# A hybrid layer on one core: eleven matmuls on zeros ahead of the first product, GLU sums and head copies in another order, and an output projection in the order 3 to 7, 0, 1, 2 that keeps its last three tiles of x1 in SBUF

## The chip, the cores and the metric

The kernel runs on one core of a Trainium2 chip. A core has five engines with a queue each, in which instructions run in order: TensorE (PE), VectorE (DVE), ScalarE (ACT), GpSimd (POOL) and SyncE (SP). SP issues most DMA transfers here and POOL the rest; a transfer whose condition is not yet met holds up all that stand behind it in the queue that issues it. The metric is the device time of the whole program in microseconds (us), as the median of several executions.

## The reference

One layer with a residual stream x of 1024 tokens by 1024 channels, in three steps (float32 throughout):

```python
# 1. token mixing
h = rms_norm(x, mix_pre_g); proj = h @ w_in            # u (512), q, k, v (8 heads x 64), f_logit (8)
y_ssm = s5_mixer(u, ...)     # diagonal state space, y + d*u, g = gelu(y), g * sigmoid(g @ glu_w + glu_b)
y_fox = forgetting_attention(q, k, v, f_logit)         # causal, decay from cumsum(log_sigmoid(f))
y_mix = concat([rms_norm(y_ssm, ssm_out_g), rms_norm(y_fox, fox_out_g)])
x = x + rms_norm(y_mix @ w_out, mix_post_g)            # x1
# 2. cross-attention, 4 heads, into 256 memory tokens
x = x + rms_norm(memory_cross_attention(rms_norm(x, xa_pre_g), rms_norm(mem, mem_g), wq, wkv, wo), xa_post_g)
# 3. SwiGLU, 2816 hidden channels
h = rms_norm(x, ffn_pre_g)
x = x + rms_norm((silu(h @ w_gate) * (h @ w_up)) @ w_down, ffn_post_g)
```

## The kernel before

Tokens stand in eight tiles of 128. A float32 operand of a large product is split into a rounded part and a rest (`split`, L112: a copy on ACT, a subtraction on DVE, L113 and L115 or L117), and each product is three matmuls (`mm3`, L121: L122, L123, L124). The Python code traces instructions with priorities; a scheduler of the framework then sets the order on every engine with a timing model of its own, from the priorities, the data and the buffers that become free. So the order on an engine is not that of the code, an edit anywhere can move other instructions, and `tc.issue_after(i)` ties instructions of a block behind instruction `i` on the same engine. A tile pool hands out a fixed number of buffers for a tag (L193 for the front: `a` 2, `b` 2, `c` 3, `d` 1, `e` 1, `yt` 2); PSUM has four banks with the tag `g`, and two double banks `s` that become four banks `x` after the attention.

The stages in order of time:

- **Input projection, state-space part** (to about 60 us, L895 to L926). `x_fetch` loads the eight row tiles of the transposed x, `x_split` splits them, `u_load` loads and splits the weight of the same row, `u_part` adds 24 matmuls into eight banks. The first x tile is loaded in two halves, and the weight after them.
- **q, k, v and the state space** (to about 230 us): `in_proj` (L868), beside which `ssm` steps. `ssm_out` (L629) makes the output of the state space in two halves of four PSUM banks, each followed by a Gelu on ACT (L639), while tiles of the second half of v (`v_tiles`, L294, emptied by ACT L310) are interleaved.
- **Forgetting attention** (`fox`, L694, to about 498 us): for each head, `prepare` loads q, k and the decay and copies and splits them (L715, L716, L718); for each of eight query tiles, `scores` (L725; L733, L734, DVE L740, exponential ACT L742, scaling L747), `turn` (L750: transposes L764, copied to SBUF by DVE L767 or ACT L769 in turn), and for pairs of heads `values` (L771). `behind` (L722) ties a head's copies behind the last exponential so far; for the first head there is none. Between these steps the generator `fillers` (L962) is paced in: the rest of v, the GLU (`glu`, L653), the first part of the output projection (`out_ssm`, L826, whose rows L836 scales with the statistics r_s from `token_sums`, L233, and `rsqrt_mean`), the memory's keys and values, and half of a folded cross-attention weight (`build_a`). At the end of `glu`, `token_sums` adds up the squares with matmuls against a column of ones (L237); `glu_stats` (L688) turns the sums into r_s.
- **Output projection, attention part** (L1018 to L1040, about 498 to 566 us): for each token tile j, x and the first part of the sum (`t`, from t1_d, L1024) are loaded, eight `mm3` make the product, DVE L1031 scales and adds, ACT L1033 squares, POOL L1035 multiplies with the gain, and L1039 makes x1, which POOL's queue stores to x1_d (L1040). Beside it steps the second half of the folded weight.
- **Cross-attention** (to about 778 us): `xa_prep(j)` loads x1 of tile j (L1058) into a buffer with the tag `c`, squares it (L1061) and makes its statistics; scores, values and the feed-forward input follow. The loads are listed in `x1_read`, and `wd_sums` (L1324) ties copies of w_down in DRAM behind entries of that list.
- **Feed-forward** (to 1414 us): seven-product schemes for gate and up (`gate_up`) and for down (`DOWN`, L1505). `take`, `quarter` and `finish` empty the banks of the last products; the last one is tile (1, 3), whose lower half is squared on ACT (L1453) and multiplied with the gain on POOL (L1459), after which the statistics (L137 to L145) and the last addition (L1497) run.

The order of the output projection's buffers is set by these lines:

```python
xt = tt("c")
sp.dma_start(out=xt, in_=a["x"][ts, :])
t = tt("aab"[j % 3])
...
stC.dma_start(out=x1_d[j], in_=xt)
```

## Time and profile before

| | |
|---|---|
| time, median of 3 runs | 1423.64 us (1420.83 to 1426.41) |
| the profiled execution's own time | 1424.64 us |
| span of its profile, first to last instruction | 1422.9 us, mean granted TensorE clock 0.989 |
| busy in the span | PE 97%, weight loads 82%, DVE 67%, ACT 46%, POOL 29% |
| DMA | 234.22 MB moved, 165 GB/s on average |

The profile is of one execution. In a timeline row stand the start, the time, engine and line, operation, output and input tiles, and in brackets how long the engine had been idle before and what ended that. In a row of windows stand the stretch, then busy time and count of PE, PEld (weight loads), DVE, ACT and POOL, the granted clock, the busy share of DMA, and GB/s. SPq is SP issuing a transfer. Tiles bear the names of their buffers, so `a`, `b`, `c`, `g`, `x` are tags; a line such as L113 or L122 can be that of a helper with many callers.

### The profile page before, as it was taken

To read this page: it belongs to the slowest core of one execution; us is meant where nothing else is said; L and a number is where in the kernel's file an instruction comes from. 1 tells how busy PE (TensorE), PEld (TensorE's weight loads), DVE (VectorE), ACT (ScalarE), POOL (GpSimd) and SP (SyncE) were. 2 spreads that over 40 slices of the span, in tenths; PEclk is the share of its full clock that TensorE was granted. 3 is DMA by queue.
4 is the path that set the end of the run, shared out by engine and by line. 5 is a ranking of instruction groups with operands and counts; after the bars stand their busy time and mean duration, and the time that the engine had idled before them with its cause. 6 is when DMAs were issued, how large, how long until landed. Compare 5 with 4: busy or idle time off the path is not lost.

```text
span 1422.9 us, 20364 instructions
## 1 busy us (share of the span) xinstructions
PE 1380.0 (97%) x7342; PEld 1165.1 (82%) x7342; DVE 956.9 (67%) x1703; ACT 653.7 (46%) x1293; POOL 406.0 (29%) x428
## 2 busy tenths in 40 slices
PE   7999989899999898999999999999999999999997
PEld 6889889789888686788888788888888888888886
DVE  8839945956566676645457677787777676565565
ACT  6372336666676555533434533333333334544351
POOL 0001000013333134002021367687666661000021
PEclk9999999999999998999999999999999999999999
DMA  6324653155643758324537355554444446965544
GB/s 208 95 77 134 172 177 105 58 166 178 202 146 106 183 184 249 116 74 135 176 115 258 123 185 185 179 172 164 151 156 155 170 148 228 346 210 192 178 163 163
DMA packets 110230, 234.22 MB, mean 165 GB/s; under 512 B 11816, under 2 KB 46632, under 8 KB 110000
## 3 DMA queue, kind: packets, MB, share of 16 engines
q1 hardware_dynamic: 94496, 179.91, 39.8%
q0 software_dynamic: 15632, 53.00, 10.4%
q8 instruction: 58, 0.95, 0.3%
q14 instruction: 44, 0.36, 0.1%
HBM read 166.81 MB, written 74.71 MB: 170 GB/s over the span
## 4 chain that ended last, share of the span: by engine, by line
PE 59%; DVE 1%; ACT 0%; issue 0%; DVEq 0%; ACTq 0%
PE x L1260 17%; PE g L1260 13%; PE x L1518 7%; PE g L1518 7%; PE x L123 2%; PE x L124 2%; PE x L122 2%; PE g L122 2%; PE g L123 2%; PE g L124 2%; PE g L1048 1%; PE g L1156 1%; DVE slab L115 0%; DVE whl L115 0%; DVE c L1039 0%; DVE rst L141 0%
## 5 line engine op out<-in xcount | busy, mean ns | idle before, releaser
L1260 PE MATMUL x<-slab,op 128*128 128x512 f32 x984 | 233.2, 389 | 0.5 <-DVE op L115 0.5
L1260 PEld LDWEIGHTS x<-slab,op 128*128 128x128 f32 x984 | 184.7, 188 | 39.2 <-DVE op L115 1.0
L1260 PE MATMUL g<-slab,op 128*128 128x512 f32 x744 | 178.7, 389 | 0.0
L115 DVE TENSOR_TENSOR slab<-slab 128x1024 fp32r<-128x1024 f32 (+2 forms) x92 | 110.5, 1207 | 84.6 <-ACT slab L113 82.6
L1260 PEld LDWEIGHTS g<-slab,op 128*128 128x128 f32 x744 | 139.7, 188 | 28.9
L122 PE MATMUL g<-slab,whl 128*128 128x512 f32 (+1 forms) x416 | 151.5, 364 | 1.7 <-ACT t L958 1.3
L124 PE MATMUL g<-slab,whl 128*128 128x512 f32 (+1 forms) x416 | 148.6, 358 | 0.0
L123 PE MATMUL g<-slab,whl 128*128 128x512 f32 (+1 forms) x416 | 148.5, 357 | 0.0
L113 ACT ACTIVATE slab<-slab 128x1024 fp32r<-128x1024 f32 (+2 forms) x92 | 95.0, 1037 | 105.0 <-DMA slab<-hs_d 75.0
L1518 PE MATMUL g<-slab 128*128 128x512 f32 x462 | 126.7, 389 | 0.0
L1518 PE MATMUL x<-slab 128*128 128x512 f32 x462 | 126.7, 389 | 0.0
L1518 PEld LDWEIGHTS x<-slab 128*128 128x128 f32 x462 | 86.7, 188 | 18.0
L1518 PEld LDWEIGHTS g<-slab 128*128 128x128 f32 x462 | 86.7, 188 | 18.0
L122 PE MATMUL g<-whl,slab 128*128 128x256 f32 (+2 forms) x288 | 88.5, 313 | 8.3 <-ACT whl L113 7.3
L115 DVE TENSOR_TENSOR whl<-raw,whl 128x1024 fp32r<-128x1024 f32 (+2 forms) x61 | 71.5, 1175 | 30.9 <-ACT whl L113 30.6
L115 DVE TENSOR_TENSOR op<-slab,op 128x512 fp32r<-128x512 f32 x80 | 83.4, 1053 | 11.5 <-ACT op L113 11.3
L1336 POOL TENSOR_TENSOR wt<-wt 128x256 f32<-128x256 f32 x88 | 83.5, 949 | 21.3 <-DMA wt<-in_w_down 17.7
L122 PEld LDWEIGHTS g<-slab,whl 128*128 128x128 f32 x416 | 78.6, 189 | 12.9 <-ACT t L958 1.5
L124 PEld LDWEIGHTS g<-slab,whl 128*128 128x128 f32 x416 | 78.4, 189 | 11.6 <-DVE whl L115 0.2
L123 PEld LDWEIGHTS g<-slab,whl 128*128 128x128 f32 x416 | 78.6, 189 | 10.6
L124 PE MATMUL g<-whl,slab 128*128 128x256 f32 (+2 forms) x288 | 86.9, 302 | 0.0
L123 PE MATMUL g<-whl,slab 128*128 128x256 f32 (+2 forms) x288 | 86.8, 301 | 0.0
(384 smaller groups left out, 2903.2 us busy)
## 6 DMA issues: line engine op xcount, KB each, us to landing
hs_d<-ev POOLq DMA_DIRECT2D x77, 256.0 KB, 2.6
slab<-hs_d SPq DMA_DIRECT2D x35, 512.0 KB
wt<-in_w_down SPq DMA_DIRECT2D x44, 256.0 KB
wt_d<-wt POOLq DMA_DIRECT2D x22, 512.0 KB, 4.8
slab<-in_w_gate SPq DMA_DIRECT2D x20, 512.0 KB
slab<-in_w_up SPq DMA_DIRECT2D x20, 512.0 KB
slab<-wt_d SPq DMA_DIRECT2D x20, 512.0 KB
wd_d<-in_w_down SPq DMA_DIRECT2D x33, 256.0 KB
```

The lines of the kernel that those rows point to most:

```text
L113: first = act.activation(out=hi, in_=src, func=AF.Copy, scale=1.0 if mul is None else mul)
L115: (lo_eng or dve).tensor_tensor(out=lo, in0=src, in1=hi.bitcast(F32), op=ALU.subtract)
L122: pe.matmul(ps, lh, rh, start=first, stop=False)
L123: pe.matmul(ps, lh, rl, start=False, stop=False)
L124: pe.matmul(ps, ll, rh, start=False, stop=last)
L1048: pe.transpose(tp[:, k], src[:, (k0 + k) * P:(k0 + k + 1) * P], ident)
L1156: turned = pe.transpose(tp[:, k], h3[:, (4 * n + k) * P:(4 * n + k + 1) * P], ident)
L1260: pe.matmul(ps, x[:, k], y[:, k], start=first and k + n == 0, stop=k == 3 and n == 2, skip_group_check=not first)
L1336: pool.tensor_tensor(out=o, in0=x, in1=y, op=ALU.subtract)
L1518: pe.matmul(banks[n][j], xo[:, u, js], wo[:, v], start=ends[0] and k == 0, stop=ends[1] and k == 2, skip_group_check=onto is not None)
```

## The change

- **Front.** A tile `still` of bf16 zeros is made with a memset on DVE, and `WARM` = 11 matmuls of 128 by 512 on it go into the first bank ahead of the first product. The first half of the first x tile is loaded and split, then the first weight is loaded, then the second half.
- **Head copies.** The list `last` is now made before all stages, and the fourth Gelu of the first half of the state-space output is its first entry, so that the copies of the first head are ordered behind it. In `turn`, heads 0 and 1 copy with ACT alone.
- **GLU sums.** `token_sums` moves from `glu` into `glu_stats`, and this is called inside `out_ssm` behind the matmuls of its first two tiles, which are scaled after it.
- **Output projection.** The tiles are taken in the order 3, 4, 5, 6, 7, 0, 1, 2; x1 of the last three stays in its buffer (`kept`), is not stored, and `xa_prep` takes it from there. `x1_read` becomes a dictionary with the tiles 3 to 7, and the copies of w_down are tied behind the next tile's load.
- **Tail.** For tile (1, 3) the lower half's product with the gain goes to DVE and into a buffer of its own (`scaled`), which the last addition reads.

```diff
 HID = ("11", "12", "22", "S1", "S2", "S3", "S4")
 EVB = 13
 OPB = 10
+WARM = 11
 
 
 def bc(ap, axis, n):
...
                     for g in range(4):
                         pe.matmul(ps[:, g], U[s_][:, 4 * b + g], T[s_][:, 4 * b + g], start=True, stop=False)
                         pe.matmul(ps[:, g], SS[s_][:, 4 * b + g], mo[s_][:, 4 * b + g], start=False, stop=True)
-                    act.activation(out=go[:, b // 2].rearrange("c j (g i) -> c g j i", i=16)[:, 4 * (b % 2):4 * (b % 2) + 4],
-                                   in_=ps.rearrange("c g (j i) -> c g j i", i=16), func=AF.Gelu_apprx_tanh)
+                    g_ = act.activation(out=go[:, b // 2].rearrange("c j (g i) -> c g j i", i=16)[:, 4 * (b % 2):4 * (b % 2) + 4],
+                                        in_=ps.rearrange("c g (j i) -> c g j i", i=16), func=AF.Gelu_apprx_tanh)
+                    if (s_, b) == (0, 3):
+                        last.append(g_)
             yield
             for ft in range(2):
                 hl = slab([P, 2, S])
...
                 if h == 1:
                     ys.append(hl)
                 yield
+        ys_stat.append((sv, acc))
+
+    def glu_stats():
+        (sv, acc), = ys_stat
         token_sums(sv, acc)
-        ys_stat.append(sv)
-
-    def glu_stats():
-        sv, = ys_stat
         tables("natural_log_exp_and_others")
         rsqrt_mean(r_s, sv, 512, 4 * EPS)
 
...
                     eng.tensor_tensor(out=qs[64:128, hs], in0=qd[64:128], in1=qs[64:128, hs].bitcast(F32),
                                       op=ALU.subtract)
                     split(ka[:, 0, hs], ka[:, 1, hs], kd, lo_eng=eng)
-
-        last = []
 
         def behind():
             return tc.issue_after(last[-1].ins) if last else ExitStack()
...
                 for k in range(n):
                     pe.transpose(tp[:, k], sc[:, (k0 + k) * P:(k0 + k + 1) * P], ident)
                 o = pt[:, k0:k0 + n, odd * P:(odd + 1) * P]
-                if (t + k0 // 4) % 2:
+                if h > 1 and (t + k0 // 4) % 2:
                     dve.tensor_copy(o, tp[:, :n])
                 else:
                     act.activation(out=o, in_=tp[:, :n], func=AF.Copy)
...
             wh, wl = load_w(a["w_out_s"][cc], 256)
             for j0 in range(0, NT, 2):
                 o = t2t([P, 2, 256])
+                made = []
                 for j in range(j0, j0 + 2):
                     ts = slice(j * P, (j + 1) * P)
                     ps = g_ps([P, 256])
                     for k in range(4):
                         mm3(ps, ys[k][:, 0, ts], ys[k][:, 1, ts], wh[:, k], wl[:, k], k == 0, k == 3)
-                    act.activation(out=o[:, j - j0], in_=ps, func=AF.Copy, scale=r_s[:, j:j + 1])
+                    made.append((j, ps))
+                    if cc + j0 == 0:
+                        yield
+                        if j == 0:
+                            continue
+                        glu_stats()
+                    for jj, ps in made:
+                        act.activation(out=o[:, jj - j0], in_=ps, func=AF.Copy, scale=r_s[:, jj:jj + 1])
+                    made = []
                     if j == j0:
                         yield
                 stB.dma_start(out=t1_d.rearrange("j c d -> c j d")[:, j0:j0 + 2, cc * 256:cc * 256 + 256], in_=o)
...
             if next(g, "end") == "end":
                 return
 
-    ys, yf, gl, ys_stat, r_mem, gate, ssm_made = [], [], [], [], [], [], []
+    ys, yf, gl, ys_stat, r_mem, gate, ssm_made, last = [], [], [], [], [], [], [], []
 
     def mem_stats():
         ss = const.tile([P, 2], F32, name="ss_mem")
...
     step(gs)
     with tc.high_priority(offset=boost):
         xts = []
-        x_fetch(xts, 0, 2)
+        x_fetch(xts, 0, 0)
         xs = [[slab([P, 2, S]) for _ in range(KT // 2)] for _ in range(2)]
         xH, xL = ([x[k // 2][:, k % 2] for k in range(KT)] for x in xs)
         acc_x = tt("d")
+
+        def x_half(i):
+            cs = slice(i * 512, i * 512 + 512)
+            sp.dma_start(out=xts[0][1][:, cs], in_=a["xT"][0:P, cs])
+            return split(xH[0][:, cs], xL[0][:, cs], xts[0][1][:, cs], g_mix[:, 0:1])
+
         banks = [g_ps([P, 512]) for _ in range(4)]
         banks += [b[:, h * 512:h * 512 + 512] for b in (s_ps([P, S]) for _ in range(2)) for h in range(2)]
+        still = tt("yt", [P, 512], BF16)
+        dve.memset(still, 0.0)
+        for _ in range(WARM):
+            pe.matmul(banks[0], still[:, 0:P], still, start=True, stop=True)
+        x_half(0)
         ws = [u_load(0)]
-        x_split(xts, (xH, xL), 0, 2)
+        x_half(1)
         u_part(banks, 0, ws[0], xH[0], xL[0])
         for k in range(1, KT):
             x_fetch(xts, k)
...
         yield from glu(ys)
         mem = []
         rows = out_ssm(ys)
-        glu_stats()
+        step(rows)
+        yield
         for _ in mem_load(r_mem[0], mem):
             step(rows)
             yield
...
         wo.append(hl)
     g_mp = gain_row(0, "d")
     a1 = build_a(1)
-    for j in range(NT):
+    kept = {}
+    for n, j in enumerate((3, 4, 5, 6, 7, 0, 1, 2)):
         ts = slice(j * P, (j + 1) * P)
         xt = tt("c")
         sp.dma_start(out=xt, in_=a["x"][ts, :])
-        t = tt("aab"[j % 3])
+        t = tt("aab"[n % 3])
         for i in range(2):
             sp.dma_start(out=t[64 * i:64 * i + 64], in_=t1_d.rearrange("j (k s) d -> s k j d", s=16)[2 * j + i])
         ss4, ss, r = sm(4, "ss4"), sm(1, "ss"), sm(1, "r")
...
         dve.tensor_reduce(out=ss, in_=ss4, op=ALU.add, axis=mybir.AxisListType.X)
         rsqrt_mean(r, ss, D)
         dve.scalar_tensor_tensor(out=xt, in0=t, scalar=r, in1=xt, op0=ALU.mult, op1=ALU.add)
-        stC.dma_start(out=x1_d[j], in_=xt)
+        if j < 3:
+            kept[j] = xt
+        else:
+            stC.dma_start(out=x1_d[j], in_=xt)
 
 
     drain(a1)
...
     g_xp = gain_row(1, "d")
     r3 = const.tile([P, NT], F32, name="r3")
 
-    xT, xr, pts, x1_read = {}, {}, {}, []
+    xT, xr, pts, x1_read = {}, {}, {}, {}
 
     def xa_prep(j):
-        x1 = tt("c")
-        x1_read.append(sp.dma_start(out=x1, in_=x1_d[j]))
+        if j in kept:
+            x1 = kept.pop(j)
+        else:
+            x1 = tt("c")
+            x1_read[j] = sp.dma_start(out=x1, in_=x1_d[j])
         ss, r = sm(1, "ss"), sm(1, "rxa")
         xT[j] = whl([P, 2, KT, P])
         act.activation(out=xT[j][:, 0].rearrange("p k t -> p (k t)"), in_=x1, func=AF.Square, accum_out=ss)
...
 
         p, cs = k // 2, slice(k % 2 * 256, k % 2 * 256 + 256)
         for f, h in ((0, 0), (1, 0), (1, 1))[2 * (k % 2):2 + k % 2]:
-            with tc.issue_after(x1_read[min(2 + k // 4, 7)].ins):
+            with tc.issue_after(x1_read[min(3 + k // 4, 7)].ins):
                 sp.dma_start(out=wd_d[f, h, p], in_=a["w_down"][2 * p + f][:, h * 512:h * 512 + 512])
         w = wtp.tile([P, 2, 2, 256], F32, name="wt", tag="wt")
         for f in range(2):
...
         return [(xo[:, :, k], wo[:, :, k]) for k in range(n)]
 
     LO, HI = slice(0, 512), slice(512, 1024)
+    scaled = []
 
     def square(t, j, h, src):
         sq = bp.tile([P, 512], F32, name="sq", tag="sq")
...
 
         c = acc[t][j][:, hs]
         square(t, j, 0 if hs is LO else 1, c)
-        pool.tensor_tensor(out=c, in0=c, in1=g_fq[:, hs], op=ALU.mult)
+        if (t, j) == (1, 3) and hs is LO:
+            scaled.append(bp.tile([P, 512], F32, name="sq", tag="sq"))
+            dve.tensor_tensor(out=scaled[0], in0=c, in1=g_fq[:, hs], op=ALU.mult)
+        else:
+            pool.tensor_tensor(out=c, in0=c, in1=g_fq[:, hs], op=ALU.mult)
 
     def add(o, ps, t):
         dve.tensor_tensor(out=o, in0=ps, in1=t, op=ALU.add)
...
         rsqrt_mean(r, second, D, ahead=first)
         last = (t, j) == (1, 3)
         for hs in (LO, HI):
-            dve.scalar_tensor_tensor(out=x2[:, hs], in0=acc[t][j][:, hs], scalar=r, in1=x2[:, hs],
-                                     op0=ALU.mult, op1=ALU.add)
+            c = scaled[0] if last and hs is LO else acc[t][j][:, hs]
+            dve.scalar_tensor_tensor(out=x2[:, hs], in0=c, scalar=r, in1=x2[:, hs], op0=ALU.mult, op1=ALU.add)
             if last:
                 sp.dma_start(out=out[tile_, hs], in_=x2[:, hs])
         if not last:
```

## The prediction

> **What bounds the kernel now.** I read the page's busy line first, then the waits of TensorE (PE) in order of size, then the busy time by stretches of 100 us, and last the timeline around each large wait.
>
> ```profile
> PE 1380.0 (97%) x7342; PEld 1165.1 (82%) x7342; DVE 956.9 (67%) x1703; ACT 653.7 (46%) x1293; POOL 406.0 (29%) x428
> ```
>
> ```profile
> PE g L122 <- ACT whl L113: 7.7, 2, 7.3
> PE g L237 <- DVE d L681: 5.4, 1, 5.4
> PE x L122 <- DVE a L1031: 4.6, 2, 4.1
> PE g L637 <- ACT t L310: 3.8, 1, 3.8
> PE g L778 <- ACT slab L769: 2.2, 1, 2.2
> ```
>
> ```profile
> 600.00:700.00 100.00, 100.00 (x492) 83.73 (x491) 49.75 (x135) 39.29 (x109) 10.10 (x15) 1.00 0.34 111
> ```
>
> The busy line gives PE 1380.0 of 1422.9 us, so only some 43 us of the span are PE idle, and the waits (waiting line and what ended the wait; total us, times, longest) name half of that in four places: the start (7.3), the token sums of the GLU (5.4), the output projection (4.1) and the first matmuls of the state-space output (3.8). The third fence is a window, PE, weight loads, DVE, ACT and POOL busy, then granted clock, DMA share and GB/s: 600 to 700 is typical of all that comes after: PE busy 100.00 of 100.00. Whatever is won before 600 us therefore arrives at the end unshortened, and nothing that other engines do after 600 us can be won except at the very tail. The change touches just these four places and the tail, so I price five terms, W, A, B, C and D. A busy PE can also be slow, at half its clock; each term has a part for that.
>
> **W, the first matmuls.** Added: a memset on VectorE (DVE), eleven bf16 matmuls 512 wide on a tile of zeros before the first real one, and the first weight load is issued between the two halves of the first x tile instead of behind both.
>
> ```profile
> 2.13 0.43 SPq L259 DMA_DIRECT2D raw<-in_w_u  x1
> ...
> 6.61 0.63 ACT L113 ACTIVATE whl<-raw 128x512 fp32r<-128x512 f32 x1 [0.27 <-DMA raw<-in_w_u]
> ...
> 7.29 2.07 PE L122 MATMUL g<-whl,slab 128*128 128x512 f32 x4 [7.29 <-ACT whl L113]
> 12.58 0.40 PE L123 MATMUL g<-whl,slab 128*128 128x512 f32 x1
> ...
> 12.82 0.40 PE L124 MATMUL g<-whl,slab 128*128 128x512 f32 x1
> 7.29:12.58 5.29, 5.29 (x13) 4.13 (x13) 4.46 (x7) 4.51 (x5) 0.00 (x0) 1.00 1.00 372
> 272.21 0.68 DVE L681 TENSOR_TENSOR d<-d,t 128x512 f32<-128x512 f32 x1
> ```
>
> PE waits 7.29 us for the split of the first weights (ACT L113, 6.61 to 7.24), which waits for their load, issued at 2.13. From 7.29 to 12.58 the window counts 13 starts, the last at its edge: 12 matmuls in 5.29 us, 0.44 apart; the next two start 0.24 apart (12.58, 12.82). The clock column reads 1.00, but the spacing halves, so I take the first stretch for the half clock. Warm, the 12 would take 12 x 0.24 = 2.9 us: **2.4 us** can be won. The burst takes about 11 x 0.44 = 4.8 us. The memset has no row of its form: I bound it by nothing and by an addition of its width, 0.68 (272.21). If it is done between 1 and 2.4 us, the burst ends between 5.8 and 7.2, before 7.29, so it delays no real work; and DVE has nothing else then, as its first split waits for the x tile. The weights' load moves up by one SP issue (0.43 for the row at 2.13), and shares the queue with one half less; the split follows it, so I take 0.3 for the start. I subtract 0.2 in case the rise comes late, and take W = 2.5. Ends: 3.3 (2.4 and 0.9 for a start at once behind the burst) and 0, because DVE and ACT are busy 4.46 and 4.51 of the 5.29 us and may not keep up with a faster PE.
>
> The Trainium skill, "TensorE: Matmul & The Clock Gate", Part 1, says that the clock is released after a busy window of about 3.4 us which runs freely and does not start with the kernel. This speaks against a burst of fixed length: by that rule 4.8 us hold one whole window only in some phases; in the worst W would be the 0.3 of the earlier start, and the sum below 13.3 in place of 15.5. The 5.29 us above agrees with it, being between one window and two.
>
> **A, the state-space output.** The copies of attention head 0 (L715, L718) are now ordered behind the fourth Gelu on ScalarE (ACT).
>
> ```profile
> 199.23 0.63 ACT L715 ACTIVATE a<-d 128x512 fp32r<-128x512 f32 x1 [8.91 <-DMA d<-qk_d]
> 199.76 0.46 ACT L310 ACTIVATE t<-g,r_x 128x256 f32<-128x256 f32 x1
> ...
> 200.27 0.80 PE L637 MATMUL g<-slab 128*128 128x128 f32 x2 [3.82 <-ACT t L310]
> ...
> 203.66 2.07 ACT L639 ACTIVATE slab<-g 128x512 f32<-128x512 f32 x4 [2.14 <-PE g L637]
> 200.27:203.45 3.18, 3.18 (x15) 3.18 (x16) 0.31 (x1) 1.25 (x1) 0.55 (x1) 0.51 0.14 46
> L733 PE MATMUL s<-slab,a x14: 220/338/478, 229.8 to 257.0; 128*128 128x512 f32 x6, 128*128 128x128 f32 x3, 128*128 128x256 f32 x3, 128*128 128x384 f32 x2
> ```
>
> ACT stood 8.91 us before a copy (L715) that waits for its load; behind it in ACT's queue stands L310, 0.46 us, which empties the PSUM bank that PE's L637 needs. PE went on at 200.27 after 3.82 idle, and then ran 3.18 us at clock 0.51. With the copy behind the Gelu, L310 follows the matmuls at once: 0.5 of the wait stays, 3.3 go, and 3.18 x 0.49 = 1.6 of slow clock goes with it. **A = 4.9.** What is queued behind the new order: the four copies of head 0 and their DVE subtractions, and the first scores wait for them (L733, first at 229.8), 24 us after the four Gelus (from 203.66, 2.07). So the delay is covered; without this cover four copies of 0.63, 2.5 us, would show. Ends: 5.4 (no wait left) and 0 (the scheduler puts another waiting instruction in front of L310).
>
> **B, GLU sums and transposes of heads 0 and 1.** The sums (L237) and what hangs on them (L238, the rsqrt, the table load) move behind the first two tiles of the next product, 2 x 12 matmuls. For heads 0 and 1 the copies that alternated to DVE go to ACT.
>
> ```profile
> 272.95 1.87 PE L237 MATMUL g<-ones,d 128*128 128x1 f32 x8 [5.37 <-DVE d L681]
> 288.40 0.66 PE L764 MATMUL g<-ident,c 128*128 128x128 f32 x4 [2.01 <-ACT t L836]
> 267.50:272.95 5.45, 0.08 (x2) 0.00 (x0) 4.66 (x8) 3.28 (x6) 1.78 (x1) 0.91 0.00 0
> 272.95:278.70 5.75, 5.75 (x27) 5.75 (x28) 4.92 (x11) 4.37 (x10) 1.28 (x1) 0.50 0.19 66
> ...
> 286.40:288.40 2.00, 0.00 (x1) 0.00 (x1) 1.70 (x3) 2.00 (x6) 1.16 (x1) 1.00 0.21 80
> 288.40:292.20 3.80, 3.80 (x21) 3.80 (x22) 2.93 (x5) 2.37 (x5) 1.85 (x2) 0.59 0.79 238
> L767 DVE COPY slab<-g 128x512 f32<-128x512 f32 (+3 forms) x10 | 5.4, 540 | 2.9 <-PE g L764 2.9
> L769 ACT ACTIVATE slab<-g 128x512 f32<-128x512 f32 (+3 forms) x10 | 4.6, 457 | 1.8 <-PE g L764 1.8
> ```
>
> PE waits 5.37 us for an addition to the sum of squares (DVE L681, the 0.68 at 272.21 above), then runs 5.75 us at clock 0.50; later it waits 2.01 for a tile that needs the sums (L836), then 3.80 us at 0.59. Lost: 5.37 + 2.01 + 5.75 x 0.50 + 3.80 x 0.41 = 11.8 us. The two tiles give PE 24 x 0.12 (half the 0.24 of a 512-wide matmul, an estimate) = 2.9 us of work in the first wait. But what is late next is DVE: in the four windows, 17.00 us, it is busy 4.66 + 4.92 + 1.70 + 2.93 = 14.2. There its slack is 2.8 us; and ten of the copies taken from it are 5.4 us, of which about half (2.6) stand before this place. If DVE sets the pace, the stretch shrinks by 2.8 + 2.6 = 5.4; ACT gets ten more of about 0.46 in exchange, with 3.28 of 5.45 busy at the wait. I take **B = 5**. Ends: 11.8, everything; and -3, since two of four PSUM banks are now held until the later sums: if nothing else is won and the wait of 2.01 grows to one like the 5.37, 3.4 are lost.
>
> **C, output projection.** Order 3 to 7, 0, 1, 2; for the last three neither the store of x1 (POOL's queue) nor its reload (SP's queue) is issued: six transfers of 512 KB. The w_down copies that stood behind the reload of tile 2 now stand behind that of tile 3.
>
> ```profile
> x_d<-c POOLq DMA_DIRECT2D x16, 512.0 KB, 5.2
> 550.34 1.32 SPq L1024 DMA_DIRECT2D a<-t_d  x2
> ...
> 553.14 0.59 POOL L1040 DMA_DIRECT2D x_d<-c  x1
> 559.83 0.75 DVE L1031 SCALAR_TENSOR_TENSOR a<-x,r_f,a 128x512 f32<-128x512 f32 x1 [4.74 <-DMA a<-t_d]
> ...
> 560.63 0.80 PE L122 MATMUL x<-whl,b 128*128 128x512 f32 x1 [4.11 <-DVE a L1031]
> 556.40:560.60 4.20, 0.12 (x1) 0.00 (x0) 0.78 (x2) 0.00 (x0) 0.00 (x0) 0.77 0.87 251
> 560.60:568.80 8.20, 6.36 (x12) 3.66 (x13) 6.50 (x11) 6.68 (x18) 3.89 (x4) 0.50 0.67 201
> ```
>
> PE waits 4.11 for a PSUM bank that DVE L1031 empties, and L1031 waits for the load of the last tile's first half of the sum, issued at 550.34 and landed at 559.8. In between DMA moves 251 GB/s (window 556.40). That load stays, with the same two buffers. Gone from beside it is one store (553.14; first row, 512 KB): at 251 GB/s 2.1 us. So half of the wait goes. Behind it PE runs at 0.50 for 8.20 us. The shorter wait, 2.0, is as long as the window 286.40:288.40 above, after which the clock was 0.59; so I let the slow stretch stand, and add 0.5 for reloads that no longer precede weight loads in SP's queue. **C = 2.6.** Ends: 4.11 + 4.1 = 8.2 with wait and slow clock gone, and -2: tile 0's statistics need no load any more and may be put among the last tile's work on ACT and DVE. The moved w_down copies cost nothing: between 600 and 700 DMA is busy 0.34 of the time (third fence); uncovered, they would matter only to loads before 600.
>
> The same part of that page says that the clock falls after an idle window of about 3.4 us. The window after a wait of 2.00 us disagrees, and I go by the window. By the rule C would be 6.7, as in rival 4 below.
>
> **D, the tail.** The last half tile's product with the gain goes from POOL to DVE, into a tile of its own, beside ACT's square.
>
> ```profile
> 575.99 0.22 DVE L141 SCALAR_TENSOR_TENSOR rst<-rsy,rsv 128x1 f32<-128x1 f32 x1
> 1415.63 0.21 DVE L139 TENSOR_SCALAR rsv<-ssq,rse 128x1 f32<-128x1 f32 x1 [0.79 <-ACT sq L1453]
> 1415.68 1.26 POOL L1459 TENSOR_TENSOR acc<-acc,g_fq 128x512 f32<-128x512 f32 x1 [6.18 <-ACT sq L1453]
> ...
> 1416.20 0.76 DVE L141 SCALAR_TENSOR_TENSOR rst<-rsy,rsv 128x1 f32<-128x1 f32 x1 [0.35 <-ACT rsy L138]
> ```
>
> DVE L141 took 0.76 us while POOL's product ran (1415.68 to 1416.94), against 0.22 elsewhere (575.99). **D = 0.5**; ends 0 and 0.6. The added product on DVE, some 0.68 as the addition above, stands in DVE's wait for the square, 0.79 at 1415.63.
>
> **Sum.** 2.5 + 4.9 + 5 + 2.6 + 0.5 = 15.5 us. Against the profiled execution, 1424.64 us: 1409.1. That execution is 1.0 above the median of the runs, 1423.64, so I forecast **1408**.
>
> **Rivals.** (1) *DVE keeps the pace of the GLU stretch and the projection's load lands no earlier*: B = C = 0, and W + A + D = 7.9 remain: 1416. For it: DVE's 14.2 of 17.0; against it: 5.4 us of copies leave DVE. (2) *The burst does not raise the clock* (the change does not do what it says): W = 0.3, so 15.5 - 2.2 = 13.3, 1410. For it: stretches at half clock lasted 5.29, 3.18, 5.75 and 3.80 us here, and the burst lasts 4.8; against it: real matmuls follow at once, so any rise comes at most some 1 us into them. This is also the time that the skill's free-running window gives in its worst phase. (3) *Slower: copies of heads 0 and 1 queue on ACT.* ACT runs in order, so a copy can stand behind an exponential that waits for DVE, with PE's PSUM bank in it. PE's longest wait for such a copy is 2.2 (L778, second fence); if each of the 12 moved copies costs that, 26.4 us are lost against W + A + C + D = 10.5: 1440. It decides from 10.5 / 12 = 0.9 us a copy. Against it: ACT was busy 3.28 of 5.45 us in the wait's window. (4) *The clock stays up behind the shorter waits*: the 8.20 us at 0.50 lose no 4.1, C = 6.7 and the time is 1404; with the slow windows of B gone too (4.4 of its 11.8, B = 8) it is 1401. For it: nothing but that 2.0 us are half of 4.11; against it: the window of 0.59.
>
> **How the numbers follow.** Forecast (1405 to 1413) 0.47; rival 1 0.24, half of it on either side of 1416.5 (its own small losses may add); rival 2 0.10; rival 4 0.10; rival 3 0.07; and 0.02 for small losses that sum to no change. About 0.5%, 7.1 us, is what a measurement can tell from no change. Faster: 0.47 + 0.12 + 0.10 + 0.10 = 0.79; within 0.5%: 0.12 + 0.02 = 0.14; slower: 0.07. The range goes from 1401, the full case of rival 4, to 1419, past rival 1 by 3 for its losses and short of rival 3: rival 3, the worst of rival 1 and what B's upper end may add below stay outside, some 0.2.
>
> **What would show it.** W: the first real matmuls start near 7 us and 0.24 apart. A: L310 before any L715, PE's wait at L637 under 1 us and the clock 1.00 after it. B: L237 behind two tiles, no wait of 5 us, and DVE near full from 260 to 290. C: the wait before L1031's bank about 2 us; three x1 stores and three loads fewer. D: L141 at 0.22. Wrong it would be if the scheduler's order, made anew for the whole program, puts a waiting instruction ahead of PE's work in a place that I don't name: a PE wait of over 5 us that is not in the list above.

## The result, and the profile after

| | before | after |
|---|---|---|
| median of the runs | 1423.66 us (1420.16 to 1427.96, 20 runs) | 1419.40 us (1414.67 to 1423.43, 20 runs) |
| ratio after / before | | 0.9972, 95% interval 0.9964 to 0.9981 |
| the profiled execution's own time; its span | 1424.64; 1422.9 us | 1418.95; 1417.2 us |

The change wins 4.3 us, 0.3%: less than a third of the 15.5 of the sum, and just beyond the slow end of the range (1419). The profile after, first the busy line, then PE's waits, the six over 1.5 us and one more (as in the prediction: waiting line, what ended the wait; total us, times, longest). Line numbers are now those of the changed kernel: L113 became L114, L122 to L124 became L123 to L125, L237 L238, L637 L638, L764 L765, L778 L779, L836 L845, L958 L979, L1031 L1054.

```profile
PE 1382.1 (98%) x7353; PEld 1162.5 (82%) x7353; DVE 948.5 (67%) x1693; ACT 658.7 (46%) x1305; POOL 403.2 (28%) x424
```

```profile
PE g L779 <- ACT t L979: 4.0, 1, 4.0
PE g L123 <- ACT t L845: 3.4, 2, 2.4
PE x L123 <- ACT slab L114: 3.2, 1, 3.2
PE s L734 <- DVE nlr L741: 3.0, 1, 3.0
PE x L123 <- DVE a L1054: 1.9, 2, 1.1
PE x L123 <- ACT whl L114: 1.7, 1, 1.7
...
PE s L452 <- ACT d L176: 0.9, 1, 0.9
```

The four waits that the prediction set out from (7.3, 5.4, 4.1, 3.8) are gone or halved, and four new ones stand in the list. The sum of the busy line hides this, because the matmuls on zeros now count as busy. To see where the time went I charge each matmul its usual spacing at full clock, add these up, and compare the times at which both kernels have done the same amount of work (the zeros count as none). The difference is the lead (us; a minus is a lag). It is an estimate: where the two kernels have the same work in another order, it moves by 1 to 3 us with what the narrow matmuls are charged.

| work done, us | 20 | 100 | 200 | 240 | 310 | 320 | 370 | 460 | 480 | 600 |
|---|---|---|---|---|---|---|---|---|---|---|
| time in the kernel before | 30.1 | 113.5 | 223.6 | 266.9 | 362.6 | 375.6 | 442.0 | 550.9 | 582.3 | 705.2 |
| lead of the changed kernel | 3.5 | 2.2 | 7.1 | 7.4 | 8.8 | 1.6 | 1.4 | 1.3 | 4.6 | 4.5 |

Up to 310 us of work the lead grows about as W and A were priced. Then some 7 us are lost, most of them at 354 to 374 us of the changed kernel, in a place that the prediction doesn't name; the rows below show 5.7 us there (4.01 idle, 1.7 of slow clock). The longer of the new waits for L845 (2.4 us, ends at 415) comes next. How the loss splits between the two places depends on the charges; together with the wait for L114's `slab` (ends at 483) they leave a lead of 1.3 to 1.7 at 460 us of work. The output projection then brings 3.3, and the tail the rest of the 5.7 us by which the two profiled executions differ.

**W and A.** The timeline's rows (start, time, engine and line, tiles; in brackets the idle time before and its end):

```profile
1.19 4.08 PE L923 MATMUL g<-yt 128*128 128x512 bf16 x11 [1.19 <-DVE epsc L96]
...
4.63 0.63 ACT L114 ACTIVATE whl<-raw 128x512 fp32r<-128x512 f32 x1
...
5.31 1.19 PE L123 MATMUL g<-whl,slab 128*128 128x512 f32 x4
...
6.34 0.39 PE L124 MATMUL g<-whl,slab 128*128 128x512 f32 x1
...
6.57 0.39 PE L125 MATMUL g<-whl,slab 128*128 128x512 f32 x1
```

```profile
194.05 0.47 ACT L311 ACTIVATE t<-g,r_x 128x256 f32<-128x256 f32 x1 [7.40 <-PE g L125]
...
194.57 0.49 PE L638 MATMUL g<-slab 128*128 128x128 f32 x2 [0.56 <-ACT t L311]
...
196.44 2.06 ACT L640 ACTIVATE slab<-g 128x512 f32<-128x512 f32 x4 [0.62 <-PE g L638]
...
198.36 0.65 ACT L718 ACTIVATE a<-e 128x512 fp32r<-128x512 f32 x1
```

```profile
195.12:200.00 4.88, 4.42 (x38) 4.23 (x37) 0.95 (x2) 3.80 (x7) 0.24 (x1) 1.00 0.29 84
```

The first real matmul starts at 5.31 instead of 7.29, because the split of the first weights (L114) starts at 4.63 instead of 6.61. From the second on the real matmuls are 0.23 apart: in this execution the half clock is spent on the zeros. Of the 3.5 us, 1.3 are given back at 74 to 81 us, where PE now comes too early for the state-space's parameters (among them its wait L452, 0.9). L310, now L311, runs at 194.05 ahead of the copies of head 0 (198.36); PE waits 0.56, and the clock behind it is 1.00.

**B.** The same 27 us of both kernels, 7 us apart as the lead says (stretch, then busy us of PE, PEld, DVE, ACT and POOL, the clock, DMA share, GB/s), and the waits around the sums; the first fence is of before, the others of after:

```profile
265.00:292.00 27.00, 19.26 (x111) 17.04 (x110) 24.03 (x53) 19.76 (x41) 6.08 (x4) 0.82 0.29 91
```

```profile
270.89 0.79 PE L734 MATMUL s<-slab,a 128*128 128x512 f32 x1 [3.01 <-DVE nlr L741]
...
273.34 1.87 PE L238 MATMUL g<-ones,d 128*128 128x1 f32 x8 [0.25 <-DVE d L684]
```

```profile
258.00:285.00 27.00, 20.82 (x123) 17.52 (x123) 26.00 (x54) 21.98 (x46) 6.10 (x4) 0.81 0.38 110
270.00:280.00 10.00, 8.22 (x33) 7.24 (x34) 9.97 (x23) 7.96 (x18) 3.44 (x2) 0.53 0.39 114
```

The wait of 5.37 before the sums is 0.25 now. But PE waits 3.01 for the score reduction of DVE (L741) just ahead of them, and then runs at 0.53 for ten us. DVE, from which the copies of two heads were taken (12 of its 48), is busier than before: 26.00 of 27.00 us against 24.03.

**The loss that the prediction doesn't have.** SP's issues and the engines around 360 us, of before, then of after (`raw<-in_w_out_s` is the load of a slice of the first half of the output projection; its split on ACT is the row `whl<-raw`):

```profile
365.65 0.33 SPq L158 DMA_DIRECT2D raw<-in_w_out_s  x1
366.81 0.45 SPq L711 DMA_DIRECT2D e<-qk_d  x1
```

```profile
370.68 1.06 ACT L113 ACTIVATE whl<-raw 128x1024 fp32r<-128x1024 f32 x1 [0.29 <-DMA raw<-in_w_out_s]
```

```profile
362.00:383.00 21.00, 20.68 (x173) 17.91 (x172) 13.15 (x30) 14.35 (x31) 6.36 (x6) 1.00 0.72 227
```

```profile
356.49 0.38 SPq L797 DMA_DIRECT2D slab<-v_d  x1
...
358.26 1.70 SPq L159 DMA_DIRECT2D raw<-in_w_out_s  x1
```

```profile
367.79 1.06 ACT L114 ACTIVATE whl<-raw 128x1024 fp32r<-128x1024 f32 x1 [5.76 <-DMA raw<-in_w_out_s]
368.75 0.36 ACT L979 ACTIVATE t<-g 128x256 f32<-128x256 f32 x1
...
369.17 3.34 PE L779 MATMUL g<-slab 128*64 128x256 f32 x16 [4.01 <-ACT t L979]
```

```profile
353.00:374.00 21.00, 16.99 (x131) 13.76 (x130) 10.59 (x23) 9.18 (x21) 2.77 (x3) 0.92 0.74 231
364.88:369.17 4.29, 0.28 (x4) 0.08 (x2) 0.29 (x1) 1.38 (x3) 0.00 (x0) 1.00 0.65 259
369.17:374.23 5.06, 5.06 (x32) 3.28 (x33) 1.25 (x3) 1.76 (x5) 0.61 (x1) 0.66 0.69 179
```

```profile
raw<-in_w_out_s SPq DMA_DIRECT2D x4, 512.0 KB
slab<-v_d SPq DMA_DIRECT2D x2, 1024.0 KB
```

Before, the third load of that weight is issued at 365.65, ahead of the next head's q and k (366.81); its split on ACT waits 0.29 and starts at 370.68, 5.0 us later. After, the same load is issued at 358.26 behind q and k and behind the second half of v, 1024 KB (L797, 356.49); its split starts at 367.79, 9.5 us later. Behind the split in ACT's queue stands the copy of a memory tile (L979), which empties the bank that PE's next product (L779) needs: ACT idle 5.76, PE idle 4.01, then 5.06 us at clock 0.66. At the 259 GB/s of the window 364.88, the 1 MB of v takes 4.0 us, about the difference of 9.5 and 5.0. The Trainium skill, "DMA: Bandwidth & Descriptors", Queues, rings and completion order, says that each DMA engine consumes the descriptors of one issuer's ring in order; by that rule a load waits for the bytes ahead of it, and these two durations agree. PE is busy 20.68 of 21.00 us there before, and 16.99 after. In the kernel before, the load that stands behind v is the fourth one (issued at 370.57). Its split comes 11.3 us later (381.85), but ACT comes to it straight from other work and doesn't wait for it.

Why the load moved: the moved sums cost the generator `fillers` one step more (`step(rows); yield`), so that everything after them in it stands one attention step later.

**C and D.**

```profile
555.82 0.50 PE L123 MATMUL x<-whl,b 128*128 128x512 f32 x1 [0.81 <-DVE a L1054]
...
557.92 0.50 PE L123 MATMUL x<-whl,b 128*128 128x512 f32 x1 [1.12 <-DVE a L1054]
...
560.62 2.02 PE L123 MATMUL x<-whl,b 128*128 128x512 f32 x4 [1.74 <-ACT whl L114]
```

```profile
556.40:564.60 8.20, 4.99 (x14) 2.93 (x13) 6.60 (x11) 6.69 (x16) 2.76 (x2) 0.79 0.29 78
```

```profile
1411.93 0.22 DVE L142 SCALAR_TENSOR_TENSOR rst<-rsy,rsv 128x1 f32<-128x1 f32 x1 [0.35 <-ACT rsy L139]
```

The tail of before, then of after (the last square, the last additions, the stores' issue):

```profile
1414.88 0.63 ACT L1453 ACTIVATE sq<-acc 128x512 f32<-128x512 f32 x1 [6.20 <-DVE acc L1462]
...
1417.19 1.42 DVE L1497 SCALAR_TENSOR_TENSOR x<-acc,r,x 128x512 f32<-128x512 f32 x2
1417.97 0.99 SPq L1500 DMA_DIRECT2D out_dram<-x  x2
```

```profile
1410.61 0.63 ACT L1483 ACTIVATE sq<-acc 128x512 f32<-128x512 f32 x1 [6.19 <-DVE acc L1496]
...
1413.05 0.75 DVE L1532 SCALAR_TENSOR_TENSOR x<-acc,r,x 128x512 f32<-128x512 f32 x1
1413.16 1.00 SPq L1534 DMA_DIRECT2D out_dram<-x  x2
```

In the changed kernel C's wait of 4.11 is two of 0.81 and 1.12, and the clock in the 8.20 us around them is 0.79, where the 8.20 us behind the wait had 0.50. D's L141, now L142, takes 0.22. From the square's start to the end of the last addition pass 1413.80 - 1410.61 = 3.19 us instead of 1418.61 - 1414.88 = 3.73, and from there to the end of the span 3.4 instead of 4.3.

### The profile page after: what moved, and what is told of

The parts are those of the page before. It is cut to its first block, busy times and chain, and to the rows that moved or that the text cites. A ratio compares the mean times of both kernels' runs of the same rounds, so it can differ in the third digit from the quotient of the medians.

```text
span 1417.2 us, 20364 instructions
## 1 busy us (share of the span) xinstructions
PE 1382.1 (98%) x7353; PEld 1162.5 (82%) x7353; DVE 948.5 (67%) x1693; ACT 658.7 (46%) x1305; POOL 403.2 (28%) x424
## 4 chain that ended last, share of the span: by engine, by line
PE 59%; DVE 1%; ACT 0%; issue 0%; DVEq 0%; ACTq 0%
PE x L1289 17%; PE g L1289 13%; PE x L1552 7%; PE g L1552 7%; PE x L125 2%; PE x L124 2%; PE x L123 2%; PE g L123 2%; PE g L125 2%; PE g L124 2%; PE g L1074 1%; PE g L1185 1%; DVE slab L116 0%; DVE whl L116 0%; DVE c L1062 0%
## 5 line engine op out<-in xcount | busy, mean ns | idle before, releaser
L123 PE MATMUL g<-slab,whl 128*128 128x512 f32 (+1 forms) x416 | 151.7, 365 | 1.1 <-ACT t L979 0.7
L125 PE MATMUL g<-slab,whl 128*128 128x512 f32 (+1 forms) x416 | 148.7, 358 | 0.0
L124 PE MATMUL g<-slab,whl 128*128 128x512 f32 (+1 forms) x416 | 148.4, 357 | 0.0
L114 ACT ACTIVATE slab<-slab 128x1024 fp32r<-128x1024 f32 (+2 forms) x92 | 94.9, 1037 | 106.3 <-DMA slab<-hs_d 82.7
L116 DVE TENSOR_TENSOR op<-slab,op 128x512 fp32r<-128x512 f32 x80 | 86.4, 1091 | 11.6 <-ACT op L114 11.4
L123 PE MATMUL g<-whl,slab 128*128 128x256 f32 (+2 forms) x288 | 86.1, 307 | 5.0 <-ACT t L845 3.4
L123 PEld LDWEIGHTS g<-slab,whl 128*128 128x128 f32 x416 | 78.6, 189 | 12.2 <-ACT t L979 0.9
L125 PEld LDWEIGHTS g<-slab,whl 128*128 128x128 f32 x416 | 78.4, 189 | 11.8 <-DVE whl L116 0.2
L124 PEld LDWEIGHTS g<-slab,whl 128*128 128x128 f32 x416 | 78.6, 189 | 10.6
L114 ACT ACTIVATE op<-slab 128x512 fp32r<-128x512 f32 x80 | 50.0, 627 | 78.5 <-PE x L1289 36.8
L124 PE MATMUL g<-whl,slab 128*128 128x256 f32 (+2 forms) x288 | 85.7, 298 | 0.0
```

The source lines that it names most:

```text
L114: first = act.activation(out=hi, in_=src, func=AF.Copy, scale=1.0 if mul is None else mul)
L116: (lo_eng or dve).tensor_tensor(out=lo, in0=src, in1=hi.bitcast(F32), op=ALU.subtract)
L123: pe.matmul(ps, lh, rh, start=first, stop=False)
L124: pe.matmul(ps, lh, rl, start=False, stop=False)
L125: pe.matmul(ps, ll, rh, start=False, stop=last)
```

## The experiments

Theory 1: the fillers' later step is what gives the lead back, and, narrower, through the load just shown. Theory 2: a resource of the attention ends it at a fixed time whatever was won ahead. Theory 3: the scheduler's order changes with any edit, and the stalls move by chance. Each ratio below is to the kernel before on the same chip, with its 95% interval.

**The step.** `phase_back` takes the empty step out, `yield_alone` puts one into the kernel before, `no_sums_move` has the sums where they were, `no_act_copies` lets the copies of heads 0 and 1 alternate again.

```diff
 # phase_back (on after)
         step(rows)
-        yield
         for _ in mem_load(r_mem[0], mem):
 # yield_alone (on before)
         glu_stats()
+        yield
 # no_sums_move (on after); out_ssm as before, token_sums in glu
-        step(rows)
-        yield
+        glu_stats()
 # no_act_copies (on after)
-                if h > 1 and (t + k0 // 4) % 2:
+                if (t + k0 // 4) % 2:
```

> The changed kernel (1419.4 us) with one thing taken out: the empty step that the fillers take behind the first tile of the first output product, so that the memory's tiles, the later rows of that product and build_a stand against the same attention steps as before. Theory 1, the later step is what gives back 7.3 us between 343 and 390 us (loads of the next w_out_s slice land behind the copies that empty PE's banks): those come back, 1412, and PE has no wait of over 2 us between 340 and 390 us. Theory 2, a resource of the attention (ACT, DVE or the loads) ends it at a fixed time and eats any lead: 1419, the lead still gone by 400 us. Theory 3, any edit reorders and moves the stalls by chance: anywhere between 1410 and 1425, with stalls at other lines.

> The kernel before (1423.7 us) with one empty step of the fillers behind the GLU statistics and nothing else. Theory 1: the later phase alone costs what the changed kernel gave back, 7.3 us: 1431, with waits of PE between 350 and 390 us for L958's copies. Theory 2: no lead, nothing eaten: 1424 within 1.5. Theory 3: a change of some us in either direction with stalls at other lines.

> The changed kernel with the GLU sums put back where they were (in glu, and the statistics ahead of the first output product); copies of heads 0 and 1 stay on ACT. The wait of 5.4 us before the sums returns, and the lead of 7.0 us at 240 us of work stays at about 7.0 instead of 8.7. Theory 1: the fillers are in their old phase, so the 7.3 us are not given back: 1419.4 + 1.7 - 7.3 = 1414. Theory 2: the lead is eaten by 400 us in any case: 1419.

> The changed kernel with the transposes' copies of heads 0 and 1 alternating between DVE and ACT again. My prediction's B put 2.6 us of its 5 on these copies. If that holds, the stretch from 255 to 300 us is 2.6 us longer: 1422. If DVE was not what the sums' place waited for, the stretch is the same, and the time is 1419 within 1. The stalls at 343 to 390 us stay by theory 1, since the fillers' step is as in the changed kernel.

| | median, us | ratio | lead at 240, 310, 320, 530 us of work |
|---|---|---|---|
| phase_back | 1419.90 | 0.9976 (0.9967 to 0.9986) | 7.8, 3.6, 2.2, 1.1 |
| yield_alone | 1429.55 | 1.0050 (1.0033 to 1.0067) | 0.9, -0.7, -7.7, -3.2 |
| no_sums_move | 1415.24 | 0.9939 (0.9924 to 0.9955) | 7.9, 9.5, 8.0, 8.8 |
| no_act_copies | 1418.95 | 0.9969 (0.9956 to 0.9981) | 7.8, 8.5, 1.4, 4.8 |

PE's waits of `yield_alone` and of `phase_back`:

```profile
PE g L778 <- ACT t L958: 3.6, 1, 3.6
```

```profile
PE g L765 <- ACT t L845: 5.0, 1, 5.0
```

The empty step alone, in the kernel before, makes the same wait (3.6; L778 and L958 are L779 and L979 of the changed kernel) and costs 7.1 us by the ratio: theory 1, and against theory 2, since there was no lead to eat. With the sums back, only 1.5 of lead goes at 310 to 320, and the time is over 4 us better than the changed kernel's. `phase_back` missed its 1412. Only 1.4 of lead goes at 310 to 320 here too, but PE waits 5.0 us for the copies behind the sums, and half of the lead is gone already at 310; two products and then the sums now fall into neighbouring steps, which is the likely reason and wasn't tried by itself. (Its profiled execution, 1422.67 us, is the slowest of its twelve, so its leads read low.) The copies on ACT, 2.6 us in my sum, are worth nothing that can be measured (0.9969 against 0.9972).

**The load.** `v_later` requests the second half of v eight attention steps later and leaves the orders of PE, DVE and POOL as they were; `yield_v_later` does it in `yield_alone`.

```diff
-                if (h, t) == (3, 5):
+                if (h, t) == (4, 5):
                     load_v(1)
```

> The changed kernel (1419.4 us) with one load moved: the second half of v is requested eight attention steps later, at tile 5 of head 4 instead of head 3; the orders of PE, DVE and POOL stay as they are. Theory 1 in its narrower form: in the changed kernel the third load of w_out_s (issued at 358.26) stands behind the next head's q and k loads and shares the DMA engines with this load of v, takes 9.4 us instead of 5.0, its split on ACT waits 5.76 us, and PE waits 4.01 us for a copy behind that split and then runs at half clock. With v's load gone from there the wait shrinks to 2 us or less and 4 to 7 us come back: 1413 to 1415. If the q and k loads ahead of it are what delays it, or ACT is late for another reason, the wait stays near 4 us: 1419.

> The kernel before with the fillers' empty step (1429.6 us) and the second half of v requested at tile 5 of head 4 instead of head 3. Theory 1 in its narrow form (the later step costs because one load of w_out_s then shares the DMA engines with this load of v): most of the 5.8 to 7.3 us come back, 1423 to 1425, and PE's wait of 3.62 us for L958 shrinks below 1.5. If the step costs by itself (other work late by one step), it stays at 1428 or more.

`v_later`: 1414.63 us, 0.9930 (0.9918 to 0.9942). `yield_v_later`: 1424.88 us, 1.0005 (0.9991 to 1.0020). The rows of `v_later`:

```profile
359.02 0.53 SPq L159 DMA_DIRECT2D raw<-in_w_out_s  x1
```

```profile
364.23 1.06 ACT L114 ACTIVATE whl<-raw 128x1024 fp32r<-128x1024 f32 x1 [0.57 <-PE g L125]
```

```profile
354.00:375.00 21.00, 21.00 (x178) 17.91 (x177) 13.94 (x32) 13.70 (x31) 4.68 (x5) 1.00 0.64 189
```

The load's split starts 5.2 us after the issue and waits for no DMA; PE is busy 21.00 of 21.00 us, where it was 16.99. From 0.9972 to 0.9930 are 6.0 us of 1423.7, and the empty step costs 0.7 instead of 7.1 us (1.0005 and 1.0050). In `yield_alone` the load takes 9.1 us to its split, in `yield_v_later` 5.3, and the wait for L958 is no longer in PE's list. So nearly all of what the step costs comes from this one load behind that of v (the collision). The loads of q and k stand ahead of it in `v_later` too, so they are not what delays it. Whether it waits behind v's bytes or shares the DMA engines with them, these runs don't tell apart. Theory 3 falls with it as far as this loss goes: two kernels lose it with the load in this place, and lose it no more when one transfer of 1 MB goes elsewhere.

**The parts.** `front_and_gelu` is W and A alone in the kernel before, `order_kept` C alone. `without_b` is the changed kernel without B, and `phase_exact` has B but with every later filler in its old step. `copies_v_later` and `without_b_v_later` are `no_sums_move` and `without_b` with the later v.

```diff
 # phase_exact (on after)
-        step(rows)
-        yield
         for _ in mem_load(r_mem[0], mem):
...
                 stB.dma_start(out=t1_d.rearrange("j c d -> c j d")[:, j0:j0 + 2, cc * 256:cc * 256 + 256], in_=o)
-                yield
+                if cc + j0:
+                    yield
```

> The kernel before with the parts W (matmuls on zeros, first weight between the halves) and A (head 0 behind the fourth Gelu) alone. The changed kernel's trace has 2.4 us for W and 4.9 for A at 240 us. Theory 1: with the fillers in the old phase nothing is given back: 1423.7 - 7.3 = 1416.4. Theory 2, a resource of the attention ends it at a fixed time: the lead is gone by 400 us, 1423.

> The kernel before with part C alone (order 3 to 7, 0, 1, 2, last three tiles of x1 kept). My sum had 2.6 for it, the changed kernel's trace 3.2: 1421 to 1420.5. If C's gain in the changed kernel came from the other state of the queues there, 1424.

> The changed kernel with the GLU sums still behind two tiles, but so that every later filler stands in its old step: the products of the first two tiles go one in each step as before, and the sums, the statistics and the two copies go with the third tile's product. Theory 1: the third load of w_out_s is issued ahead of the next head's loads again, and no 7.3 us are given back: 1412 to 1413. If the sums' place itself costs (they now hold two banks longer, as in rival 3's line of thought), 1415 or more, the time of the changed kernel without the moved sums.

> The changed kernel without the whole of part B: sums in their old place, copies of heads 0 and 1 alternating again; W, A, C and D stay. From the parts: W and A 7.1, C between 1.3 (its timed run) and 3.0 (its trace), D 1.4 (by the tails of the traces): 1423.8 - 9.8 to 11.5 = 1412.3 to 1414. My prediction's sum without B would be 10.5: 1413. If the copies on ACT are worth the 1.7 us by which the wait before the sums is shorter with them (3.6 instead of 5.4), it is 1417 (1415.2 + 1.7).

> The changed kernel without the moved sums (1415.2 us) and with v's second half requested at tile 5 of head 4. Here the third load of w_out_s is ahead of the next head's loads already, so the narrow theory gives little: 1415 within 1.5. A gain of 4 us or more would say that v's load costs elsewhere too, and that the gain of the later v in the changed kernel isn't all the collision's.

> W, A, C and D without B, and v's second half requested at tile 5 of head 4: a version that may beat both kernels. By the narrow theory the same as without_b within 1.5, 1412 to 1415; if v's load costs elsewhere, 1410 or less.

| | sums | copies | v | median, us | ratio |
|---|---|---|---|---|---|
| front_and_gelu (W, A) | old | old | old | 1417.51 | 0.9954 (0.9941 to 0.9967) |
| order_kept (C) | old | old | old | 1423.49 | 0.9991 (0.9980 to 1.0001) |
| without_b (W, A, C, D) | old | old | old | 1416.00 | 0.9940 (0.9922 to 0.9957) |
| without_b_v_later | old | old | later | 1415.42 | 0.9936 (0.9920 to 0.9951) |
| no_sums_move | old | ACT | old | 1415.24 | 0.9939 (0.9924 to 0.9955) |
| copies_v_later | old | ACT | later | 1415.15 | 0.9932 (0.9916 to 0.9947) |
| phase_exact | new, old step | ACT | old | 1416.23 | 0.9944 (0.9931 to 0.9957) |
| v_later | new | ACT | later | 1414.63 | 0.9930 (0.9918 to 0.9942) |

W and A are 6.5 us (4.7 to 8.4): the lead isn't eaten, theory 2 falls. C is 1.3 (-0.1 to 2.8) by the times, so `order_kept` missed its 1420.5 to 1421. (Its profiled execution, 1418.89 us, is the fastest of its twelve.) The lead grows over C's stretch, from 450 to 490 us of work, by between -0.7 and 3.4 us in the traces that have C, most often about 1.8. But it grows by some 1.5 and 2.3 in `yield_alone` and `yield_v_later` too, which have the old order. PE's wait for the projection's bank, which the tile's scaling empties (L1031 of the kernel before, here under each kernel's own number), with C in `without_b` and without C in `yield_alone`:

```profile
PE x L123 <- DVE a L1044: 5.2, 2, 4.8
PE x L122 <- DVE a L1032: 2.8, 2, 1.7
```

The longest such wait is 1.1 to 4.8 us in the twelve traces with C, and 1.7 to 4.1 in the four without: it changes with what came before, and no run shows which part of a shorter wait is C's.

The last six rows are the same within their intervals, whether the sums are moved, the copies are on ACT, or neither. From `without_b_v_later` to `v_later`, which differ by B alone, are 0.9 us (about -2 to 4): B is worth nothing that can be measured, and not the 5 of the sum. `without_b` missed its 1412.3 to 1414 by 2, `without_b_v_later` its 1415 by 0.4. `phase_exact` missed its 1412 to 1413; it was expected at 1415 or more if the new place of the sums itself costs, but beside the other rows such a cost is within the intervals. Where the load doesn't collide, a later v brings 0.6 and 1.0 us by the ratios, within the intervals.

**Why B brings nothing.** Two more kernels, on `v_later`, take work from DVE in B's stretch:

```diff
 # glu_add_pool
-                dve.tensor_tensor(out=y, in0=gl[ct][:, 0, hs].bitcast(F32), in1=gl[ct][:, 1, hs].bitcast(F32), op=ALU.add)
+                pool.tensor_tensor(out=y, in0=gl[ct][:, 0, hs].bitcast(F32), in1=gl[ct][:, 1, hs].bitcast(F32), op=ALU.add)
 # scale_pool
-            if t in POOL_T and h > 1:
+            if t in POOL_T and h > 0:
```

> The kernel with v's second half later (1414.6 us, all parts of the change in it), with the eight additions of the GLU's two halves of g on POOL in place of DVE: DVE loses eight operations of 0.68 us, 5.4 us, ahead of and within the stretch from 225 to 275 us. Part B was to be worth 5 us there and its traces show nothing. Rival 1's reading, DVE keeps the pace of the stretch: PE's losses between 260 and 290 us (14.8 in the changed kernel) shrink by 3 to 5 us, 1410 to 1412. If not DVE's amount of work but the chain to the sums and their statistics (additions, sums, rsqrt, copies, one behind the other) keeps the pace, the losses stay at 14 to 16: 1414.6 within 1.5.

> The kernel with v's second half later (1414.6 us), with the scaling of three query tiles of head 1 (tiles 1, 3 and 5) on POOL in place of DVE; PE's order stays. It takes some 1.5 us off DVE between 270 and 300 us, but in a chain in which POOL is slower. If DVE keeps the pace there: 1 us won, 1413.6. If the chains do: 1415 to 1417, as each of the three tiles is later.

`glu_add_pool`: 1411.89 us, 0.9921 (0.9909 to 0.9933), the lowest ratio of these runs, 11.2 us better than the kernel before. `scale_pool`: 1413.07 us, 0.9924 (0.9911 to 0.9938). Their differences from `v_later`, 1.3 and 0.9 us, are within the intervals. The trace of `glu_add_pool`, a window of the stretch and its largest wait there, beside the same window of `v_later`:

```profile
255.00:280.00 25.00, 19.73 (x115) 17.26 (x113) 24.20 (x52) 20.34 (x44) 8.71 (x6) 0.80 0.23 70
```

```profile
PE s L734 <- DVE nlr L741: 2.4, 1, 2.4
```

```profile
255.00:280.00 25.00, 20.19 (x116) 16.93 (x114) 24.09 (x53) 20.00 (x42) 6.09 (x4) 0.80 0.24 65
```

Its lead over `v_later` is 3.2 us at 280 us of work and 1.9 at 490. So 5.4 us less of work on DVE won 3.2 in the stretch, and DVE is still busy 24.20 of 25.00 us (24.09 in `v_later`), with other work moved up. This fits rival 1's reading, that DVE keeps the pace. But the additions also stand in the chain that leads to the sums, and `scale_pool`, which takes three scalings from DVE behind that place, leads `v_later` by only 0.1 at 280 us of work. So that B brings nothing is shown; that the amount of DVE's work is the reason is likely and not shown.

## Why the prediction was right and where it was wrong

- **W, 2.5: right in size, partly by luck.** The first matmul came at 5.31, not near 7: the earlier start was worth 2.0 where the sum had 0.3. With the 2.4 of the clock that is 4.4, of which 3.5 were left at 20 us of work; 1.3 were lost again at 74 to 81 us, and 2.2 remained. Rival 2 (the burst doesn't raise the clock) is out: 0.23 apart. The Trainium skill, "TensorE: Matmul & The Clock Gate", Part 1, has a busy window of about 3.4 us, of free phase, for the rise. In the clock records of the changed kernel's trace the rise comes at 4.34, 3.15 us behind the burst's start; in the twelve traces with the burst it comes 2.8 to 6.0 us behind it, which agrees with a free phase, though 2.8 is less than one such window.
- **A, 4.9: right**, in size and in each row named: lead from 2.2 to 7.1, L311 first, wait 0.56, clock 1.00. W and A together were 7.4 in the sum and 6.5 (4.7 to 8.4) in the runs.
- **B, 5: wrong, by all of it.** The step that failed is "If DVE sets the pace, the stretch shrinks by 2.8 + 2.6 = 5.4": it took the slack of DVE in four windows for time that PE would win. The wait before the sums did go; DVE, nearly full already, filled the freed time with the scores that stood behind, and PE's wait moved to them (3.01, L734 for L741). Rival 1 had B = 0, and its mechanism fits this stretch; B = 0 was also within the ends.
- **The missing term: -6.0.** The change's description says that the sums go behind two tiles; that this makes the generator one step longer, I priced at nothing and never followed into SP's queue. There it put a load of 512 KB behind one of 1024 KB that nobody was waiting for. The sum without B and with this term is 15.5 - 5 - 6.0 = 4.5; measured 4.3. That they are so close is luck in part: with the measured 6.5 for W and A, 1.3 for C and 1.4 for the tail it is 3.2. The prediction's own sign for such a place, a PE wait of over 5 us that it doesn't name, set the bound too high: the wait was 4.01, and with the slow clock behind it 5.7 were lost.
- **C, 2.6: not shown.** Three x1 stores and three loads are gone (16 to 13, 8 to 5), and in the changed kernel the wait is 1.9 in place of 4.1, as forecast. But the times give 1.3 (-0.1 to 2.8), with C the wait is 4.8 in `without_b`, and without C it is 1.7 in `yield_alone`. The slow stretch got milder, which half of rival 4 had said.
- **D, 0.5: right on the chain, short at the end.** From the last square to the last addition 3.19 us pass, not 3.73: 0.54. Another 0.9 is won behind it; see the last section. Rival 3 (copies queue on ACT) is out: without the copies on ACT the time is the same.

The forecast of faster by over 0.5% failed with these two terms: the change is 0.3% faster. Free of the collision (`v_later`) it is 0.7% faster.

## What to carry to other kernels

When work is woven from generators that step against each other, an added step moves every later load against loads of other owners: list what each queue issues next to what, before and after, and ask of each load whether its first consumer stands in front of something urgent. A stage in which another engine is nearly full (here DVE, 24 of 27 us) may not give back a wait that is taken out of it: look first at what that engine will do in the freed time. Move large transfers that nobody needs soon away from small ones that someone waits for: here one condition in one line was worth 6 us, more than B, C and D together.

## What the runs showed of the hardware

- The end of the program: from the start of the last square to the end of the span 7.8 to 8.0 us pass in the five profiles without D, and 6.6 in those with it. Of the 1.4 only 0.5 lie on the chain that I priced. The rest is in the closing signals: POOL's comes 0.8 to 1.1 us behind SP's last one where POOL made the last product, and 0.03 behind it where DVE made it. The runs don't tell why.
- The zeros raised the clock for what follows as real data do. In the twelve traces with the burst at most three real matmuls start before the spacing is full (0.22 to 0.24 us), in the four without it twelve to fourteen. In four of the twelve the rise came at 4.0 to 4.8 us, with matmuls of the burst still to go (4.34 in the changed kernel); in the other eight at 5.5 to 7.2, in the burst's last matmul or behind it.
- In all sixteen traces the clock records change on one grid: each half-clock stretch between the start and the tail lasts one to four times 3.41 us, and the full-clock stretches between them are whole multiples too. So each such piece costs 1.7 us (half of 3.41) of work at full clock; the collision's is one piece, at 369.57.
